# Routing of a mixture of experts in batches of tiles, the first gathers ahead of the weight splits, and a rare branch moved to the end

## The chip, the cores and the metric

The kernel runs on one core of a Trainium2 chip. The metric is the device time of one execution in microseconds (us). The engines that matter here are TensorE (PE, with its weight loads PEld), VectorE (DVE), ScalarE (ACT), GpSimd (POOL) and SyncE (SP, which here issues plain DMAs only).

## The reference

Two transformer-like blocks run one after the other on a sequence of S = 2048 rows of D = 1024. The change touches only the last part of the second: the hierarchical mixture of experts, with 4 groups of 8 experts, two experts for a row, and hidden width 256.

```python
def hierarchical_moe(h, w_rg, b_rg, w_re, b_re, w_gate, w_up, w_down):
    t = h.reshape(N, D)
    g_prob = softmax(t @ w_rg + b_rg)
    g_p, g_idx = lax.top_k(g_prob, 1)
    e_logits = (t @ w_re + b_re).reshape(N, N_GROUPS, EXPERTS_PER_GROUP)[chosen group]
    e_p, e_idx = lax.top_k(softmax(e_logits), TOP_K)
    weights = g_p * e_p / sum(e_p)
    expert = g_idx * EXPERTS_PER_GROUP + e_idx
    ...
    hid = silu(xb @ w_gate[e]) * (xb @ w_up[e])
    y[rows of e] += weights * (hid @ w_down[e])

def hybrid_layer(...):
    ...
    x = x + gate1 * (mixed @ w_out)
    h2 = rms_norm_2(x, norm2_g) * (1.0 + scale2) + shift2
    return x + gate2 * hierarchical_moe(h2, ...)
```

## The kernel before, in words

The time up to 2444 computes the first block and the attention and recurrence of the second, and is the same before and after. What follows has three parts.

**The routing stage** (`p6`, L1898) goes over the 16 tiles of 128 rows. For a tile, `operand` (L1930) splits the mixed activations into a high and a low part, `main` (L1937) multiplies them with `w_out` on PE (three products for one, L98 to L100, in a rounded 32-bit form) and adds each half of the result to the residual on DVE (L1946, four adds a tile), then normalizes the row (L1950 to L1955) and writes it to device memory, `h_d`, from which the experts gather. `router` (L1959), one tile behind, transposes the normalized rows (L1964), copies them (L1965), multiplies them with the router's weights (L1968, 16 instructions of 40 columns) and adds the bias (`lg`, L1970). `route` (L2012) then works on that one tile with some 37 small DVE instructions: the best group, the two best experts of it, their weights, and each row's rank in its expert's list, for which PE multiplies the choice with a triangular matrix (L2048) and the running count with ones (L2050). `place` (L2071) turns rank and expert into one-hot matrices R (128 x 128) and A (three groups of 128 columns: the token, and the weight's high and low part), and PE sums R times A into the lists of all experts in one PSUM bank (L2079), which has four columns for each expert: up to four blocks of 128 rows of its own.

**Between the routing stage and the experts** stands `route_end` (L2096): it counts the blocks of each expert (`nbi`, L2101 to L2105), makes the row indices `sidx` and weights `roww` from the bank (`row_lists`, L2081), the last block's index and weight of each expert (`lsidx`, `lroww`), and the number of blocks beyond four (`tli`). Then comes a branch, `If(nt > 0)` (L2128), with the lists for experts of more than four blocks, some 465 instructions, which this input does not take. `experts` (L2157) then clears five row buffers on POOL (L2167), splits the first expert's weights into high and low parts (`split_expert`, L2256: ACT casts at L2265, DVE subtracts at L2266), gathers the first two experts' rows (L2273, an indirect DMA that POOL issues) and transposes the first (L2285).

**The expert loop** (L2179 to L2202) is unrolled over 32 experts. Its order on PE, ACT, DVE and POOL is the program's own (a manual schedule); everything ahead of it is ordered by a planner that has costs and due times of each instruction. SP's queue is ordered by the planner throughout. Within an iteration, all engines load the number of the expert's blocks, `nb`, from `nbi` into a register (L2179), POOL gathers rows ahead, PE does half of the up and gate products of this expert, the turn and down product of the expert before (L2307, L2321), and the other half. A branch `If(nb > 1)` (L2198) holds the second to fourth blocks; 20 of the 32 experts don't take it. The results go to the output by a scatter that adds (L2323). Behind the loop a register load (L2203) and a loop over blocks beyond four (L2204) end the kernel; this input has none.

Of the kernel before, what the change touches and what calls it, by code (L numbers as in the profile page):

```python
# [20 lines left out]
P = 128  # L21
S = 2048
# [8 lines left out]
def f32(ap):  # L31
    return ap.bitcast(F32)
# [28 lines left out]
class Kernel:  # L61
# [11 lines left out]
    LATE = 15.5  # L73
    AHEAD = 3
# [44 lines left out]
    def build(self):  # L119
        tc, nc = self.tc, self.nc  # L120
        with ExitStack() as ctx:
            self.cst = cst = ctx.enter_context(tc.tile_pool(name="cst", bufs=1, reuse_waits="tile"))
# [1752 lines left out]
    def route_tiles(self, ctx):  # L1875
# [7 lines left out]
        self.nbi, self.tli = t("nbi", 32, dt=I32), t("tli", 40, dt=I32)  # L1883

        self.rk, self.ek, self.wk = t("rk", NT, 2, 2), t("ek", NT, 2), t("wk", NT, 2)
        self.io = t("io", P)
# [11 lines left out]
    def p6(self):  # L1898
        tc, nc, a = self.tc, self.nc, self.a
        V = nc.vector  # L1900
        with ExitStack() as ctx:

            qp = self.pools(ctx, "qp", ("cnt", "br", "v4", "r4", "rst_o", "lg", "mxl", "hT", "wr", "mx", "hx", "x1", "mxh", "sq", "sh2", "gn2"))
            t = lambda nm, *w, dt=F32, bufs=1: qp.tile([P, *w], dt, name=nm, bufs=bufs)

            cnt = t("cnt", 32, dt=F32R)
            V.memset(f32(cnt), 0.0)
# [29 lines left out]
            def main(n, mh, ml, r2):  # L1937
# [9 lines left out]
                nc.sync.dma_start(self.out[n * P:n * P + P, :], x)  # L1947
                hx = t("hx", D, bufs=2)
# [10 lines left out]
            def router(n, hx):  # L1959
# [12 lines left out]


            order = [4 * q + i for q in (3, 2, 1, 0) for i in range(4)]
# [22 lines left out]
            for i, n in enumerate(order):  # L1997
# [11 lines left out]
            router(order[-1], hx)  # L2009
            self.route_end(qp, cnt, rows)  # L2010

    def route(self, rp, n, lg, cnt, rows, first, last):  # L2012
# [3 lines left out]
        t = lambda nm, *w, dt=F32, bufs=2: rp.tile([P, *w], dt, name=nm, bufs=bufs)  # L2016
        U32 = mybir.dt.uint32

        g8, gi, gf = t("g8", 8), t("gi", 8, dt=U32), t("gf", 1)
        V.max(g8, lg[:, :8])  # L2020
        V.max_index(gi, g8, lg[:, :8])
        V.tensor_copy(gf, gi[:, 0:1])
        nm, ge, gs = t("nm", 1), t("ge", 8), t("gs", 1)
        V.tensor_scalar(nm, g8[:, 0:1], -1.0, None, op0=OP.mult)
        nc.scalar.activation(ge, lg[:, :8], AF.Exp, bias=nm, accum_out=gs)
        V.reciprocal(gs, gs)

        oh, el = t("oh", 4), t("el", 32)
        V.tensor_scalar(oh, self.io[:, :4], gf, -1e30, op0=OP.not_equal, op1=OP.mult)
        V.tensor_tensor(el.rearrange("p (g e) -> p g e", g=4), lg[:, 8:].rearrange("p (g e) -> p g e", g=4),  # L2030
                        oh[:, :, None].to_broadcast([P, 4, 8]), OP.add)
        m8, x8 = t("m8", 8), t("x8", 8, dt=U32)
        V.max(m8, el)
        V.max_index(x8, m8, el)
        e, w, d = self.ek[:, n], self.wk[:, n], t("d", 1)
        V.tensor_copy(e, x8[:, :2])
        V.tensor_tensor(d, m8[:, 0:1], m8[:, 1:2], OP.subtract)
        nc.scalar.activation(d, d, AF.Tanh, scale=0.5)
        V.tensor_scalar(gs, gs, 0.5, None, op0=OP.mult)
        V.scalar_tensor_tensor(w[:, 0:1], d, 1.0, gs, op0=OP.add, op1=OP.mult)  # L2040
        V.tensor_scalar(d, d, -1.0, 1.0, op0=OP.mult, op1=OP.add)
        V.tensor_tensor(w[:, 1:2], d, gs, OP.mult)

        M, Ms = t("M", 2, 32), t("Ms", 32, dt=F32R)
        V.tensor_tensor(M, self.io[:, None, :32].to_broadcast([P, 2, 32]), e[:, :, None].to_broadcast([P, 2, 32]), OP.is_equal)
        V.tensor_tensor(Ms, M[:, 0], M[:, 1], OP.add)
        pr = self.bank("aux")
        nc.tensor.matmul(pr[:, :32], self.low, Ms, start=True, stop=first)  # L2048
        if not first:
            nc.tensor.matmul(pr[:, :32], self.one, cnt, start=False, stop=True)  # L2050
        V.tensor_tensor(M, M, pr[:, None, :32].to_broadcast([P, 2, 32]), OP.mult)
        V.tensor_tensor(cnt, cnt, Ms, OP.add)
        vf, vi, ri = t("vf", 2), t("vi", 2, dt=I32), t("ri", 2, 2, dt=I32)
        V.tensor_reduce(vf, M, mybir.AxisListType.X, OP.add)
        V.tensor_copy(vi, vf)
        V.tensor_scalar(ri[:, 0], vi, 127, None, op0=OP.bitwise_and)
        V.tensor_scalar(ri[:, 1], vi, 7, None, op0=OP.arith_shift_right)
        rk = self.rk[:, n]
# [3 lines left out]
        V.tensor_scalar(cl, rk[:, 1], 4.0, 1000.0, op0=OP.is_ge, op1=OP.mult)  # L2062
        V.scalar_tensor_tensor(cl, e, 4.0, cl, op0=OP.mult, op1=OP.add)
        V.tensor_tensor(cl, cl, rk[:, 1], OP.add)
        wr, wl = t("wr2", 2, dt=F32R), t("wl2", 2)
        V.tensor_copy(wr, w)
        V.tensor_tensor(wl, w, f32(wr), OP.subtract)
        for k in range(2):
            self.place(rp, n, k, cl[:, k:k + 1], P, wr, wl, rows, first and k == 0, last and k == 1)

    def place(self, rp, n, k, col, w, wr, wl, rows, start, stop):  # L2071

        nc = self.nc
        R = rp.tile([P, P], F32R, name="R", bufs=2)
        nc.vector.tensor_scalar(R, self.io, self.rk[:, n, 0, k:k + 1], None, op0=OP.is_equal)
# [5 lines left out]
    def row_lists(self, rp, rows, c0, w):  # L2081

        V = self.nc.vector
        t = lambda nm, dt=F32: rp.tile([P, w], dt, name=f"{nm}{w}")
        cs = slice(c0, c0 + w)
        r, z = t("rl"), t("rz")
        V.tensor_scalar(r, rows[:, :w], -1.0, None, op0=OP.add)
        pd = rp.tile([P, 1], F32, name="pd")
        V.tensor_scalar(pd, self.pid, float(S + 1), None, op0=OP.add)
        V.tensor_scalar(z, r, 0.0, pd, op0=OP.is_lt, op1=OP.mult)  # L2090
        V.tensor_tensor(r, r, z, OP.add)  # L2091
        V.tensor_copy(self.sidx[:, cs], r)  # L2092
        V.tensor_copy(self.roww[:, cs], rows[:, w:2 * w])
        V.tensor_tensor(self.roww[:, cs], self.roww[:, cs], rows[:, 2 * w:3 * w], OP.add)
# [261 lines left out]
```

## Time and profile before

| | us |
|---|---|
| median of 3 runs | 3287.71 (3283.44 to 3288.76) |
| the profiled execution | 3284.43 |
| its span | 3282.3 |
| PE busy | 2997.3 (91%) |
| DVE busy | 2226.2 (68%) |
| ACT busy | 1533.3 (47%) |
| POOL busy | 903.8 (28%) |
| granted PE clock, mean | 0.964 |

The span is that of the profiled execution, the time from its first to its last instruction; the execution itself took 2.1 us more. Busy times are the time in which an engine had an instruction in work. In the rows below, a time in brackets is how long the engine stood idle ahead of the instruction, with the instruction, or the queue step of an engine (a name with q), that ended the idle time. "128*128 128x512" is the stationary and the moving operand of a product. [...]

### The profile page before, as it was taken

To read this page: it belongs to the slowest core of one execution; us is meant where nothing else is said; L and a number is where in the kernel's file an instruction comes from. 1 tells how busy PE (TensorE), PEld (TensorE's weight loads), DVE (VectorE), ACT (ScalarE), POOL (GpSimd) and SP (SyncE) were. 2 spreads that over 40 slices of the span, in tenths; PEclk is the share of its full clock that TensorE was granted. 3 is DMA by queue.
4 is the path that set the end of the run, shared out by engine and by line. 5 is a ranking of instruction groups with operands and counts; after the bars stand their busy time and mean duration, and the time that the engine had idled before them with its cause. 6 is when DMAs were issued, how large, how long until landed. Compare 5 with 4: busy or idle time off the path is not lost. (4 is left out here: it accounts for less than half of the span.)

```text
span 3282.3 us, 43935 instructions
## 1 busy us (share of the span) xinstructions
PE 2997.3 (91%) x14243; PEld 2403.5 (73%) x14243; DVE 2226.2 (68%) x4948; ACT 1533.3 (47%) x3020; POOL 903.8 (28%) x868
## 2 busy tenths in 40 slices
PE   7999999989998788899999789899999986999997
PEld 5778779968876667777888667687877764666665
DVE  4356764448786996537666698888877886674463
ACT  4332331146665543225555677666554543452332
POOL 0003550012223531443343553222200002342232
PEclk9999999999998899999999899999999988999999
DMA  5534557653637878684544521223253327996682
GB/s 171 181 83 145 188 186 233 213 137 115 201 104 204 250 226 263 208 268 146 154 135 130 131 90 55 82 66 91 69 192 131 129 96 269 291 347 190 172 261 42
DMA packets 411128, 545.44 MB, mean 166 GB/s; under 512 B 73953, under 2 KB 263745, under 8 KB 409826
## 3 DMA queue, kind: packets, MB, share of 16 engines
q1 hardware_dynamic: 392850, 508.41, 48.4%
q0 software_dynamic: 18000, 33.60, 4.6%
q8 instruction: 141, 2.31, 0.3%
q14 instruction: 137, 1.12, 0.1%
HBM read 393.00 MB, written 180.84 MB: 175 GB/s over the span
## 5 line engine op out<-in xcount | busy, mean ns | idle before, releaser
L98 PE MATMUL fm<-h,wh 128*128 128x512 f32 x960 | 388.0, 408 | 7.9 <-ACT ev L234 5.7
L99 PE MATMUL fm<-h,wh 128*128 128x512 f32 x960 | 384.0, 400 | 0.0
L100 PE MATMUL fm<-h,wl 128*128 128x512 f32 x960 | 381.5, 398 | 0.6 <-DVE wl L91 0.6
L98 PEld LDWEIGHTS fm<-h,wh 128*128 128x128 f32 x960 | 182.9, 191 | 47.8 <-ACT ev L234 7.7
L100 PEld LDWEIGHTS fm<-h,wl 128*128 128x128 f32 x960 | 182.5, 190 | 41.2 <-DVE wl L91 1.0
L99 PEld LDWEIGHTS fm<-h,wh 128*128 128x128 f32 x960 | 182.9, 191 | 31.8
L98 PE MATMUL mm<-wegh,xh 128*128 128x512 f32 x376 | 169.6, 451 | 25.7 <-ACT g L2299 24.6
L2321 PE MATMUL mm<-wd,st 128*128 128x512 f32 x368 | 167.3, 597 | 9.4 <-ACTq L2229 5.0
L2266 DVE TENSOR_TENSOR wegl<-wf,wegh 128x1024 fp32r<-128x1024 f32 x128 | 151.1, 1223 | 6.1
L2299 ACT ACTIVATE g<-mm 128x256 f32<-128x256 f32 x47 | 18.0, 383 | 290.3 <-PEq L2198 98.0
L91 DVE TENSOR_TENSOR tl<-tr,th 128x512 fp32r<-128x512 f32 (+2 forms) x204 | 130.8, 644 | 30.5 <-ACT th L90 29.7
L100 PE MATMUL mm<-wegh,xl 128*128 128x512 f32 x376 | 148.6, 395 | 0.0
L99 PE MATMUL mm<-wegl,xh 128*128 128x512 f32 x376 | 147.9, 393 | 0.0
L861 POOL TENSOR_TENSOR q<-q,q 64x512 fp32r<-64x512 f32 x32 | 43.3, 1355 | 366.3 <-ACT q L860 286.1
L90 ACT CAST th<-tr 128x512 fp32r<-128x512 f32 (+2 forms) x204 | 110.2, 548 | 43.6 <-PE tr L902 18.5
L2265 ACT CAST wegh<-wf 128x1024 fp32r<-128x1024 f32 x128 | 127.7, 1049 | 3.4 <-DVE nf L2108 3.2
L2321 PEld LDWEIGHTS mm<-wd,st 128*128 128x128 f32 x368 | 66.3, 190 | 79.5 <-issue 65.0
L2300 DVE SCALAR_TENSOR_TENSOR g<-g,mm 128x256 f32<-128x256 f32 x47 | 19.8, 421 | 144.7 <-ACT g L2299 144.7
L98 PEld LDWEIGHTS mm<-wegh,xh 128*128 128x128 f32 x376 | 71.3, 190 | 60.9 <-ACT g L2299 37.5
L98 PE MATMUL mm<-wo,mxh 128*128 128x512 f32 x256 | 105.1, 410 | 8.0 <-DVE x L1946 5.2
L2323 POOL DMA_INDIRECT out_y<-y,lsidx x32 | 51.6, 1613 | 193.0 <-DVEq L2198 119.7
L99 PE MATMUL mm<-wo,mxh 128*128 128x512 f32 x256 | 104.3, 407 | 0.0
(707 smaller groups left out, 9178.4 us busy)
## 6 DMA issues: line engine op xcount, KB each, us to landing
wf<-in_w_gate SPq DMA_DIRECT2D x64, 512.0 KB
wf<-in_w_up SPq DMA_DIRECT2D x64, 512.0 KB
wd<-in_w_down SPq DMA_DIRECT2D x62, 512.0 KB
wa<-in_w_ada SPq DMA_DIRECT2D x96, 256.0 KB
w<-in_w_in SPq DMA_DIRECT2D x43, 512.0 KB
g_d<-Gs SPq DMA_DIRECT2D x32, 544.0 KB
G<-g_d SPq DMA_DIRECT2D x32, 544.0 KB
x<-in_x SPq DMA_DIRECT2D x32, 512.0 KB
```

The source lines that it names most:

```text
L90: nc.scalar.copy(hi, src)
L91: nc.vector.tensor_tensor(lo, src, f32(hi), OP.subtract)
L98: mm(ps, lh, rh, start=start, stop=False)
L99: mm(ps, lh, rl, start=False, stop=False)
L100: mm(ps, ll, rh, start=False, stop=stop)
L861: nc.gpsimd.tensor_tensor(q[64:], q2[64:], f32(q[64:]), OP.subtract)
L2265: nc.scalar.copy(hi, f)
L2266: nc.vector.tensor_tensor(lo, f, f32(hi), OP.subtract)
L2299: nc.scalar.activation(g, pm[:, :256], AF.Tanh, scale=0.5)
L2300: nc.vector.scalar_tensor_tensor(g, g, 1.0, pm[:, :256], op0=OP.add, op1=OP.mult)
L2321: nc.tensor.matmul(po, st[:, k * P:k * P + P], wts[1][k][:, hs], start=k == 0, stop=k == 1)
L2323: nc.gpsimd.indirect_dma_start(out=self.out, out_offset=bass.IndirectOffsetOnAxis(ap=sidx, axis=0), in_=y, in_offset=None, compute_op=OP.a ...
```

## The change

1. Routing works in batches of tiles, 4, 4, 4, 3 and 1: `router` leaves the logits of a tile in a common tile, and `route` works on the whole batch with operands of three dimensions; two searches, one one-hot and four columns of A remain for each tile. The rank products run once for a batch, over 32 columns for each tile of it; the running counts are kept for all tiles.
2. `place` uses R and A in plain 32-bit floats instead of the rounded form, so the weight needs no low part: A has 2 x 128 columns instead of 3 x 128. The token numbers start at minus 2048, so `row_lists` has two DVE instructions instead of seven.
3. `router` of the last but one tile comes ahead of the last tile's `main`. From behind that `main` to the end of the experts, PE, ACT, DVE and POOL are in the program's order.
4. The branch for experts of more than four blocks moves from `route_end` to the end of the kernel, joined with the loop over such blocks. `lsidx`, `lroww` and `tli` are made in `route_last`, behind the first expert's transposes.
5. The first two row buffers are cleared and gathered into ahead of the other three and of the first expert's splits.
6. `nb` is loaded just ahead of its branch instead of at the start of the iteration.

```diff
+    BATCH = ((0, 4), (4, 8), (8, 12), (12, 15), (15, 16))
...
+        self.cnt = t("cnt", NT + 1, 32, dt=F32R)
...
-        nc.gpsimd.iota(self.tok, pattern=[[P, NT]], base=1, channel_multiplier=1, allow_small_or_imprecise_dtypes=True)
+        nc.gpsimd.iota(self.tok, pattern=[[P, NT]], base=-S, channel_multiplier=1, allow_small_or_imprecise_dtypes=True)
...
-                lg = t("lg", 40, bufs=2)
-                V.tensor_tensor(lg, pl[:, :40], br, OP.add)
-                self.route(qp, n, lg, cnt, rows, n == order[0], n == order[-1])
+                b = next(b for b, (lo, hi) in enumerate(self.BATCH) if lo <= i < hi)
+                lo, hi = self.BATCH[b]
+                if i == lo:
+                    lgs[b] = t("lg", 4, 40, bufs=2)[:, :hi - lo]
+                V.tensor_tensor(lgs[b][:, i - lo], pl[:, :40], br, OP.add)
+                if i == hi - 1:
+                    self.route(qp, order, lo, hi, lgs.pop(b), rows)
...
-                h2 = main(n, *cur)
-                if hx is not None:
-                    router(order[i - 1], hx)
+                if i == NT - 1:
+                    router(i - 1, hx)
+                x = main(n, *cur)
+                if i == NT - 1:
+
+                    self.given = self.ctx.enter_context(ExitStack())
+                    self.given.enter_context(tc.manual_schedule(engines={getattr(mybir.EngineType, k) for k in (
+                        "PE", "Activation", "DVE", "Pool")}))
+                h2 = norm(n, x)
+                if 0 < i < NT - 1:
+                    router(i - 1, hx)
...
+        pr = self.bank("aux")
+        nc.tensor.matmul(pr[:, :32 * B], self.low, Ms.rearrange("p b e -> p (b e)"), start=True, stop=False)
+        nc.tensor.matmul(pr[:, :32 * B], self.one, self.cnt[:, lo:hi].rearrange("p b e -> p (b e)"), start=False, stop=True)
...
+        for i in range(B):
+            R = rp.tile([P, 2, P], F32, name="R", bufs=2)
+            self.one_hot(R, rk[:, i, 0])
+            for k in range(2):
+                self.place(rp, order, lo + i, k, R[:, k], cl[:, i, k:k + 1], P, rows, lo + i + k == 0, lo + i + k == NT)
...
-        A = rp.tile([P, 3, w], F32R, name=f"A{w}", bufs=2)
-        for j, v in enumerate((self.tok[:, n:n + 1], f32(wr)[:, k:k + 1], wl[:, k:k + 1])):
+        A = rp.tile([P, 2, w], F32, name=f"A{w}", bufs=2)
+        n = order[i]
+        for j, v in enumerate((self.tok[:, n:n + 1], self.wk[:, i, k:k + 1])):
             nc.vector.tensor_scalar(A[:, j], self.io[:, :w], col, v, op0=OP.is_equal, op1=OP.mult)
-        nc.tensor.matmul(rows[:, :3 * w], R, A.rearrange("p a b -> p (a b)"), start=start, stop=stop)
+        nc.tensor.matmul(rows[:, :2 * w], R, A.rearrange("p a b -> p (a b)"), start=start, stop=stop)
...
+        V.tensor_scalar(self.sidx[:, cs], rows[:, :w], float(S), None, op0=OP.add)
         V.tensor_copy(self.roww[:, cs], rows[:, w:2 * w])
...
-        for x in self.xg + self.xo:
+        for e in range(2):
+            nc.gpsimd.memset(self.xg[e], 0.0)
+            self.gather(self.xg[e], 4 * e)
+        for x in (self.xo[0], self.xg[2], self.xo[1]):
             nc.gpsimd.memset(x, 0.0)
         wts, steps = self.split_expert(self.wf)
         for f in steps:
             f()
-        for e in range(2):
-            self.gather(self.xg[e], 4 * e)
         xt = self.expert_x(ep, self.xg[0])
+        self.route_last(ep)
         wf = self.load_expert(self.expert_src(1))
...
-                nb = nc.values_load(self.nbi[0:1, e:e + 1], min_val=0, max_val=16)
...
+            nb = nc.values_load(self.nbi[0:1, e:e + 1], min_val=0, max_val=16)
+            with tc.If(nb > 1):
+                self.expert_over(ep, wts, e, nb, 1, pm)
...
+        self.given.close()
         nt = nc.values_load(self.tli[0:1, 32:33], min_val=0, max_val=32)
+        with tc.If(nt > 0):
+            self.expert_tail(ep, nt)
```

## Rows read from the trace of the kernel before

**Rows 1.** Busy time by stretch; columns: stretch, us, each engine's busy us, PEclk, DMA share, GB/s

```profile
2444.00:2680.00 236.00, 226.07 (x1156) 187.79 (x1154) 187.86 (x742) 115.34 (x175) 0.95 (x1) 0.96 0.36 134
2677.30:2735.90 58.60, 23.32 (x93) 18.65 (x90) 42.77 (x204) 12.22 (x25) 7.98 (x8) 0.53 0.49 174
2736.00:3272.00 536.00, 489.83 (x1967) 333.45 (x1966) 308.71 (x403) 199.76 (x308) 170.14 (x121) 0.99 0.73 227
```

**Rows 2.** Waits of PE in the routing stage, 2444 to 2680: total, times, longest

```profile
PE mm L98 <- DVE x L1946: 5.2, 4, 3.3
```

**Rows 3.** PE in order of time through the seam: start us, us, instruction, idle before

```profile
2676.68 0.40 PE L99 MATMUL mm<-wo,mxh 128*128 128x512 f32 x1
2676.91 0.40 PE L100 MATMUL mm<-wo,mxl 128*128 128x512 f32 x1
...
2692.25 1.09 PE L1964 MATMUL tr<-ident,hx 128*128 128x128 f32 x4
2694.02 1.12 PE L1964 MATMUL tr<-ident,hx 128*128 128x128 f32 x4 [0.68 <-ACT hT L1965]
...
2698.52 3.61 PE L1968 MATMUL aux<-wr,hT 128*128 128x40 f32 x16
...
2734.11 1.94 PE L2285 MATMUL tr<-ident,xg 128*128 128x128 f32 x8 [16.51 <-DMA xg<-h_d,sidx]
2735.88 0.80 PE L98 MATMUL mm<-wegh,xh 128*128 128x512 f32 x1
```

**Rows 4.** DVE in order of time through the seam

```profile
2679.58 3.49 DVE L2266 TENSOR_TENSOR wegl<-wf,wegh 128x1024 fp32r<-128x1024 f32 x3
2682.98 0.75 DVE L1946 SCALAR_TENSOR_TENSOR x<-mm,r,x 128x512 f32<-128x512 f32 x1
...
2702.31 0.20 DVE L1970 TENSOR_TENSOR lg<-aux,br 128x40 f32<-128x40 f32 x1
...
2709.31 0.20 DVE L1970 TENSOR_TENSOR lg<-aux,br 128x40 f32<-128x40 f32 x1
...
2716.52 0.34 DVE L2078 TENSOR_SCALAR A<-io,cl,wl 128x128 fp32r<-128x128 f32 x1
...
2727.54 0.29 DVE L2091 TENSOR_TENSOR rl<-rl,rz 128x128 f32<-128x128 f32 x1 [5.86 <-DVEq L2128]
2727.87 0.68 DVE L2092 CAST sidx<-rl 128x128 int32<-128x128 f32 x1
...
2745.79 3.50 DVE L2266 TENSOR_TENSOR wegl<-wf,wegh 128x1024 fp32r<-128x1024 f32 x3
```

**Rows 5.** POOL in order of time, two issues of a gather

```profile
2729.45 1.23 POOL L2273 DMA_INDIRECT xg<-h_d,sidx  x1 [0.98 <-DVE lc L2116]
...
2745.85 2.03 POOL L2273 DMA_INDIRECT xg<-h_d,sidx  x1 [0.30 <-issue]
```

**Rows 6.** PE in order of time: a down product, and the head of an expert

```profile
2748.95 3.60 PE L2321 MATMUL mm<-wf,st 128*128 128x512 f32 x8
...
2756.00 0.47 PE L98 MATMUL mm<-wegh,xh 128*128 128x512 f32 x1 [0.71 <-ACT g L2299]
```

**Rows 7.** Waits of PE in the expert loop, 2736 to 3283: total, times, longest

```profile
PE mm L98 <- ACT g L2299: 24.6, 29, 2.1
```

**Rows 8.** Line 2179, register loads: queue, operation, count, ns min/median/max, first and last start

```profile
L2179 SPq TENSOR_LOAD <-nbi x32: 263/263/491, 2714.3 to 2737.2; - x32
...
L2179 PEldq TENSOR_LOAD <-nbi x32: 297/303/416, 2734.1 to 3253.3; - x32
```

**Rows 9.** Line 2203, the register load behind the expert loop

```profile
L2203 PEldq TENSOR_LOAD <-tli x1: 305/305/305, 3266.5 to 3266.5; - x1
```

**Rows 10.** The end in order of time, PE and POOL

```profile
3266.51 3.70 PE L2321 MATMUL mm<-wd,st 128*128 128x512 f32 x8 [0.53 <-ACT st L2309]
...
3271.28 1.57 POOL L2323 DMA_INDIRECT out_y<-y,lsidx  x1 [7.40 <-DVEq L2204]
```

**Rows 11.** Line 2204, the last loop's waits on SP's queue

```profile
L2204 SPq EVENT_SEMAPHORE  x19: 17/28/28, 3195.3 to 3277.9; - x19
```

More of the change, by code (lines that the diff above doesn't have):

```diff
@@ L2008, in p6, with route @@
                     self.wf = self.load_expert(self.expert_src(0), True)
-            router(order[-1], hx)
-            self.route_end(qp, cnt, rows)
-    def route(self, rp, n, lg, cnt, rows, first, last):
+            router(NT - 1, hx)
+            self.route_end(qp, rows)
+    def route(self, rp, order, lo, hi, lg, rows):
         nc = self.nc
         V = nc.vector
-        t = lambda nm, *w, dt=F32, bufs=2: rp.tile([P, *w], dt, name=nm, bufs=bufs)
+        B = hi - lo
+        t = lambda nm, *w, dt=F32: rp.tile([P, 4, *w], dt, name=nm)[:, :B]
+        bc = lambda x, *w: x.to_broadcast([P, B, *w])
+        X = mybir.AxisListType.X
@@ L2030, in route @@
[L2030 to L2038, printed above, removed]
+        gm, eq, e1, ge = t("gm"), t("eq", 4), t("e1"), t("ge", 4)
@@ new lines, in route @@
+        V.tensor_copy(e, x8[:, :, :2])
+        M, Ms = t("M", 2, 32), t("Ms", 32, dt=F32R)
+        V.tensor_tensor(M.rearrange("p b k e -> p (b k) e"), self.io[:, None, :32].to_broadcast([P, 2 * B, 32]),
+                        e.rearrange("p b k -> p (b k)")[:, :, None].to_broadcast([P, 2 * B, 32]), OP.is_equal)
+        V.tensor_tensor(Ms, M[:, :, 0], M[:, :, 1], OP.add)
+        for i in range(B):
+            V.tensor_tensor(self.cnt[:, lo + i + 1], f32(self.cnt)[:, lo + i], f32(Ms)[:, i], OP.add)
@@ L2063, in route @@
         V.scalar_tensor_tensor(cl, e, 4.0, cl, op0=OP.mult, op1=OP.add)
[L2064 to L2071, printed above, removed]
+        V.tensor_tensor(cl, cl, rk[:, :, 1], OP.add)
@@ L2083, in row_lists @@
+    def row_lists(self, rows, c0, w):
         V = self.nc.vector
-        t = lambda nm, dt=F32: rp.tile([P, w], dt, name=f"{nm}{w}")
         cs = slice(c0, c0 + w)
[L2086 to L2092, printed above, removed]
+        V.tensor_scalar(self.sidx[:, cs], rows[:, :w], float(S), None, op0=OP.add)
@@ L2093, in row_lists, with route_end @@
         V.tensor_copy(self.roww[:, cs], rows[:, w:2 * w])
-        V.tensor_tensor(self.roww[:, cs], self.roww[:, cs], rows[:, 2 * w:3 * w], OP.add)
-    def route_end(self, rp, cnt, rows):
+    def route_end(self, rp, rows):
         tc, nc = self.tc, self.nc
@@ L2105, in route_end, with route_last @@
         V.tensor_scalar(self.nbi, ci, 7, None, op0=OP.arith_shift_right)
-        self.row_lists(rp, rows, 0, P)
+        self.row_lists(rows, 0, P)
+    def route_last(self, rp):
+        V = self.nc.vector
+        t = lambda nm, *w, dt=F32: rp.tile([P, *w], dt, name=nm)
+        nf, one, lc, sel, sv = t("nf", 32), t("one1", 32), t("lc", 32), t("sel", 32, 4), t("selv", 32, 4)
         V.tensor_copy(nf, self.nbi)
-        lc, sel, sv = t("lc", 32), t("sel", 32, 4), t("selv", 32, 4)
         V.tensor_scalar(lc, nf, 1.0, 4.0, op0=OP.max, op1=OP.min)
@@ L2203, in experts @@
-        nt = nc.values_load(self.tli[0:1, 32:33], min_val=0, max_val=32)
+        for e in range(32):
+            self.gather(self.xo[0], 4 * e + 1)
+            if e < 30:
+                self.gather(self.xg[(e + 2) % 3], 4 * e + 8)
+            wn, steps = self.split_expert(wf) if e < 31 else (None, [])
+            split = lambda: steps and steps.pop(0)()
+            pm = self.mmps()
+            self.expert_up(pm, wts, xt, range(4))
+            s = self.expert_gate(ep, last[0]) if last else None
+            for _ in range(3):
+                split()
+            st = self.expert_turn(ep, s) if last else None
+            xn = self.expert_x(ep, self.xg[(e + 1) % 3]) if e < 31 else None
+            split()
+            if last:
+                self.expert_down(ep, last[1], st, last[2])
+            self.expert_up(pm, wts, xt, range(4, 8))
+            if e < 30:
+                wf = self.load_expert(self.expert_src(e + 2))
+            nb = nc.values_load(self.nbi[0:1, e:e + 1], min_val=0, max_val=16)
+            with tc.If(nb > 1):
+                self.expert_over(ep, wts, e, nb, 1, pm)
+            last = pm, wts, (self.lsidx[:, e:e + 1], self.lroww[:, e:e + 1])
+            wts, xt = wn, xn
```

175 lines of the change are left out of this document (83 added, 92 removed).

## The prediction

> **What bounds the kernel now.** I read the busy table by stretches first. [...] In PE's order of time the last product of the last tile ends at 2677.31 (2676.91 + 0.40) and the first expert product starts at 2735.88 [rows 3]: 58.6 us, in which PE is busy 23.3 and mostly at half clock (mean 0.53) [rows 1]. Nothing there is limited by an engine's speed; it is a chain of small steps. In the expert loop, 2736 to 3272, PE is busy 489.8 of 536 us at 0.99 [rows 1], so PE bounds again, and its largest wait is 24.6 us in 29 pieces at the head of an expert's products [rows 7]. So each part is priced in the stage where it acts.
>
> **Routing in batches.** DVE needs 7.0 us before the change for one routed tile (logits at 2702.31 and again at 2709.31, with nothing idle between) [rows 4]. A batch of four does some 40 small instructions at about 0.2 us of pitch (8 us) and, per tile, two searches, the one-hot, four columns of A at 0.26 and a count, some 2.2 us: about 16.8 us for four, 4.2 a tile. DVE saves some 40 us in all, but DVE is not the bound here. On PE the placement grows: it was two products of 384 columns in the rounded form, which at the 0.23 us between products of 512 columns (2676.68 to 2676.91) [rows 3] are 0.17 us each; now it is two of 256 columns in full F32, and full-F32 products of 512 columns take 0.45 us an instruction, two instructions each (3.60 us for 8) [rows 6], so about 0.45 for 256. That is +0.56 us a tile, +8 for 15 tiles; the rank products, issued five times instead of 16, give back about 1.4: **+6.6 us** of PE. [...] A later DVE, free of 40 us, makes the adds of L1946 sooner, but a batch also holds DVE for longer in one piece, so I take back 6. Net **+1**; bounds: all 15 come back, -8; none does and the pieces cost 3 more, +10.
>
> **The seam.** Before, behind the last product came: three weight splits of expert 0 on DVE (3.49 us from 2679.58) that held back the last add (2682.98) [rows 4]; the rest of three tiles' routing in turn, each with 16 logit products of 3.61 us at half clock (2698.52) [rows 3]; the last columns of A until 2716.86; three weight splits of expert 1; and 5.86 us in which DVE stood at the not-taken long branch, with row_lists split around it (2727.54) [rows 4]. Then the gather was issued (2729.45) [rows 5] and landed for transposes at 2734.11 [rows 3].
> After, only tile 15 is left. From the end of its product I sum: tile 14's router moved in front, 2.9 (transposes of 1.09 and 1.12 and logits of 3.61 at half clock, halved); add 0.3 + 0.75; norm from the add's end to the first transpose, 2683.73 to 2692.25, less 1.0 for the other tiles' routing between its steps: 7.5; transposes from 2692.25 to 2695.14 with the copy and hand-over behind them, 4.1; logits 3.6 + 0.4; one route alone, 2709.31 to 2716.86, 7.5 [rows 3, 4]; placement 0.9 (two of 0.45), count product 0.4, block counts and sidx 1.3 (four small steps, 0.68 for sidx among them as it was); gather from the index to landing 2728.55 to 2734.11, 5.5; transposes to the first product 1.8 [rows 3, 4]. That is 37.0, and with 1.0 for the gather (below) 38.0 against 58.6: **-21**. Bounds: the batch 12 to 14 may reach into the seam, and DVE's order may delay tile 15 by 9, so -12; if norm, transposes and route lose another fifth without such steps between, -26. The four splits of expert 0 (3.49 for three on DVE, so 1.2 each [rows 4]) now run in the gather's shadow of 5.5; should that cover be short, the first product waits for one split, 1.2. Expert 1's splits and the 14 small steps for lsidx move into the first iteration, where DVE has room: 308.7 of 536 us busy [rows 1]; 0 to +1.
> The gathers issued ahead now run beside DVE's splits. Issue by POOL took 1.23 us with DVE free (2729.45) and 2.03 beside splits (2745.85, over splits from 2745.79 to 2749.29) [rows 4, 5]: +1.0, the one in the sum. [...]
>
> **The register load.** At 29 boundaries of the loop PE stands before the next expert's first product, 24.6 us together [rows 7], 0.85 each; where no branch is taken 0.71, as at 2756.00 [rows 6]. The load of nb sits in this gap: 0.303 us on PE's queue, 32 times [rows 8]; with its dispatch about 0.41 (an estimate: a third more for the steps around it). Now it stands behind the last products, ahead of the branch that already was there. That such a load runs ahead of the array the end shows: L2203 was loaded on PE at 3266.5 [rows 9] while products went on to 3270.2 [rows 10]. 29 x 0.41 = **-12**; bounds -9 (the bare 0.303) and -14 (all but 0.37 of each gap), or 0 if it isn't hidden (rival 3). On DVE, ACT and POOL the load moves as well; ACT is busy 199.8 of 536 [rows 1], so nothing waits longer. SP's loads (32 of 0.263, each with two steps more) ran in one row from 2714 to 2737 [rows 8]; what is queued behind them on SP are the weight loads, see the rivals.
>
> **The end.** The not-taken long branch goes behind the last scatter. Its 5.86 us stand beside the landing of that scatter: issued at 3271.28 [rows 10], the final waits end at 3277.9 [rows 11]. So 0; bounds -1 and +4. [...]
>
> **Sum.** +1 - 21 - 12 + 0 = -32. The profiled execution took 3284.43 us, 3.3 below the median 3287.71. From the profiled time 3252.4, on the median's scale 3255.7; I take 3255. The forecast's own range is 3238 to 3270.
>
> **Rivals.** 1, the seam gives half: the order on PE, ACT, DVE and POOL is written by hand from the last tile's norm on, so one late step holds all behind it, and route of tiles 12 to 14 may spill some 12 us of DVE into tile 15's norm; for it speaks DVE's 42.8 of 58.6 us in the seam [rows 1]. Then -9 instead of -21, **3267**. 2, SP is not in the hand-made order: its 32 register loads (about 20 us in a row) stand ahead of expert 1's weights, and the second expert waits; against it, in steady state weights are issued far ahead. +8, **3264**. 3, the change doesn't do what it says: the load still waits for the array, for the wait for the gate lies in the same gap [rows 7]; -20 only, **3268**. [...] 5, **slower**: the batches hold DVE in pieces of 16 us where a tile of PE's work lasts 14.7 (236/16), the residual adds wait, PE's result buffers fill and PE stops. It decides from 8 us per batch: four batches are 32 and eat up all the rest; at 9 each, **3292**. Against it: DVE's order here is planned with due times, so adds pass between the small steps, and DVE has 48 us free.
>
> **How the numbers follow.** Forecast 0.62, rival 1 0.14, 2 0.07, 3 0.06, 4 0.04, 5 0.04, unnamed 0.03. The range 3237 to 3273 takes in the forecast with its bounds and rivals 1 to 4. A measurement of this kernel can tell about 0.2%, 6.6 us, from no change: faster means below 3281. All but rival 5, and far corners where the seam and the loop both fail, lie below: 0.91 faster, 0.05 same, 0.04 slower.
>
> **What would show it.** Right: the last product of the last tile to the first expert product takes 36 to 41 us; no DVE wait for the branch before sidx; PE's waits at the heads of experts fall from 24.6 to about 12; placement instructions twice as many, PE's idle in the routing stage not over 10. Wrong: PE waits for L1946 of several us in each batch; the seam over 47; a gap of 0.7 that stays although the register load has left it; the second expert's products waiting for weights.

## The result and the profile after

The changed kernel takes **3246.18 us** (median of 4 runs, 3240.00 to 3247.80) against 3285.57 for the kernel before in its 4 runs: ratio 0.9878, interval 0.9859 to 0.9896, so 39 us faster. The forecast was 3255, between 3237 and 3273. A second set of runs of the same kernel (below) gave 0.987 (0.9849 to 0.989). The sum was near; its terms were not. To see that, both profiled executions are cut at the same events: the first and the last product with `w_out`, the first and the last product of the experts. The stretches are: the routing stage, the seam, the expert loop and the end. Here is the table of busy time by stretch, first of the kernel before, then of the changed one (columns as in [rows 1]; PEclk is the granted clock, TensorE's clock as a share of its full speed):

```profile
2431.20:2677.30 246.10, 237.20 (x1199) 197.19 (x1200) 190.20 (x742) 118.69 (x176) 0.95 (x1) 0.96 0.40 145
2677.30:2735.88 58.58, 23.30 (x93) 18.63 (x90) 42.75 (x204) 12.22 (x25) 7.98 (x8) 0.53 0.49 174
2735.88:3270.20 534.32, 489.94 (x1967) 333.57 (x1966) 308.08 (x402) 199.76 (x308) 169.42 (x120) 0.99 0.74 227
3270.20:3282.30 12.10, 0.01 (x1) 0.00 (x0) 0.75 (x1) 0.00 (x0) 1.57 (x1) 0.71 0.26 40
```

```profile
2423.70:2659.30 235.60, 235.60 (x1219) 197.76 (x1220) 162.01 (x462) 85.20 (x124) 0.95 (x1) 0.99 0.41 151
2659.30:2695.72 36.42, 18.49 (x83) 14.85 (x81) 25.03 (x115) 9.34 (x16) 7.19 (x6) 0.66 0.59 209
2695.72:3229.10 533.38, 493.80 (x1967) 333.63 (x1966) 310.31 (x420) 202.56 (x311) 176.70 (x122) 0.99 0.75 233
3229.10:3238.20 9.10, 0.01 (x1) 0.00 (x0) 0.75 (x1) 0.00 (x0) 1.57 (x1) 0.76 0.36 55
```

| stretch | before | after | difference | forecast |
|---|---|---|---|---|
| ahead of the routing stage | 2431.2 | 2423.7 | -7.5 | 0 |
| routing stage | 246.1 | 235.6 | -10.5 | +1 |
| seam | 58.6 | 36.4 | -22.2 | -21 |
| expert loop | 534.3 | 533.4 | -0.9 | -12 |
| end | 12.1 | 9.1 | -3.0 | 0 |
| span | 3282.3 | 3238.2 | -44.1 | -32 |

The first line is no gain: up to 2392 PE's instructions are the same ones in the same order, and in the runs of this study the routing stage began anywhere from 2423.7 to 2433.8. Of the 9.9 us between the spans of the changed kernel's two profiled executions, 7.1 lie here. This is why single stretches are compared below, and why two kernels that are 5 us apart can't be told by their medians. In the profiled execution the changes themselves make -36.6.

**The routing stage** has PE busy without a gap, 235.6 of 235.6 us, at a clock of 0.99 instead of 0.96: the 8.9 us of idle are gone, the wait for L1946 [rows 2] among them.

**The seam** in PE's order of time (columns as in [rows 3]):

```profile
2664.32 0.63 PE L1974 MATMUL tr<-ident,hx 128*128 128x128 f32 x4 [1.13 <-DVE hx L1964]
...
2669.50 0.45 PE L2073 MATMUL aux<-Ms,low 128*128 128x96 f32 x1 [3.16 <-DVE Ms L2069]
2669.75 3.60 PE L1978 MATMUL aux<-wr,hT 128*128 128x40 f32 x16
...
2677.22 2.08 PE L2121 MATMUL aux<-A,R 128*128 128x256 f32 x4 [3.65 <-DVE A L2120]
...
2693.95 1.94 PE L2331 MATMUL tr<-ident,xg 128*128 128x128 f32 x8 [7.54 <-DMA xg<-h_d,sidx]
2695.72 0.80 PE L99 MATMUL mm<-wegh,xh 128*128 128x512 f32 x1
```

and DVE's part of it, from the last add to the row lists and the splits behind them:

```profile
2659.36 0.75 DVE L1952 SCALAR_TENSOR_TENSOR x<-mm,r,x 128x512 f32<-128x512 f32 x1 [2.03 <-PE mm L101]
...
2673.39 0.20 DVE L1983 TENSOR_TENSOR lg<-aux,br 128x40 f32<-128x40 f32 x1 [3.26 <-PE aux L1978]
...
2686.99 0.28 DVE L2127 TENSOR_SCALAR sidx<-aux 128x128 int32<-128x128 f32 x1
...
2687.39 4.62 DVE L2312 TENSOR_TENSOR wegl<-wf,wegh 128x1024 fp32r<-128x1024 f32 x4
```

The last product ends at 2659.3. The norm now goes straight through: 4.2 us from the add's end to the first transpose, against 8.5 in [rows 3, 4]. Then PE stands 3.16 us for `Ms` of the batch of tiles 12 to 14, which is ahead of the last tile's logits in the program's order; and from the logits (2673.39) to `sidx` (2686.99) DVE works 13.6 us, since it routes that batch and the last tile together. No branch is on the way; the splits (2687.39) lie behind the row lists. The first gather beside them:

```profile
2688.17 1.54 POOL L2319 DMA_INDIRECT xg<-h_d,sidx  x1 [55.82 <-DMA wd<-in_w_down]
...
2690.96 1.94 POOL L2319 DMA_INDIRECT xg<-h_d,sidx  x1 [0.28 <-POOL xg L2205]
```

From its issue to the transposes 5.8 us pass, 4.7 before [rows 3, 5]. So the +1.0 for a gather beside splits is near in this execution, but not by its reason: the issue itself is only 0.31 longer (1.54 against 1.23), and the rest lies between the issue and the transposes. In the other runs whose first gather is issued beside splits, issue to transposes takes 5.5 to 8.1 us; in e5 and e6 below, where no split runs beside it, 4.7 and 4.8. Whether the splits lengthen it or the weight transfers of the same time was not tried. The issue did not wait for the splits to end: it was over at 2689.71, while DVE's four splits ran until 2692.01.

**The expert loop** is where 11 us are missing. A head is PE's idle time ahead of an expert's first product. The heads did get shorter where nothing else is late. Two heads, the second and the third expert's (columns as in [rows 6]):

```profile
2706.20 0.47 PE L99 MATMUL mm<-wegh,xh 128*128 128x512 f32 x1 [1.76 <-DVEq L2236]
...
2716.79 0.47 PE L99 MATMUL mm<-wegh,xh 128*128 128x512 f32 x1 [0.30 <-PEq L2236]
```

The third expert's head is 0.30 instead of 0.71: the 0.41 that was forecast, to the digit; where the branch's body was run it is 0.54 instead of 0.94. But others are 0.8 to 1.8, and the sum of PE's waits at the heads is 17.0 instead of 25.7 (24.6 of these are in [rows 7]):

```profile
PE mm L99 <- PEq L2236: 6.9, 16, 1.5
PE mm L99 <- ACT g L2345: 5.8, 10, 0.8
...
PE tr L2331 <- DMA xg<-h_d,sidx: 1.0, 2, 0.8
...
PE mm L99 <- DVEq L2236: 4.3, 4, 1.8
...
PE tr L2331 <- DMA xo<-h_d,sidx: 3.6, 2, 1.9
```

**The end** is 3.0 us shorter. The branch, now L2243, does stall DVE there, for 2.9 us from 3229.5 (first and last start in each row):

```profile
L2243 DVEq COMPARE_BRANCH  x1: 56/56/56, 3229.5 to 3229.5; - x1
...
L2243 DVEq EVENT_SEMAPHORE  x1: 21/21/21, 3232.4 to 3232.4; - x1
```

It lies beside the last scatter, issued at 3230.18, which has the engines wait until 3236.6, as forecast. The 3 us come from elsewhere: the loop over blocks beyond four is now inside the branch, so its own start and end are passed over. From the scatter's landing to the span's end it took 4.9 us before and takes 1.6 now. Before, every engine's queue went through the loop's waits behind the landing (1.3 us, [rows 11] for SP's), and only then could POOL begin the step that ends its queue (DRAIN), which took 2.8 us. Now that step begins at 3231.7, beside the landing, and is over 0.8 us behind it. POOL's step before and after (count, ns min/median/max, first and last start; the longest is the first):

```profile
L2352 POOLq DRAIN  x3: 46/103/2763, 3278.7 to 3282.0; - x3
```

```profile
L2398 POOLq DRAIN  x3: 46/113/5731, 3231.7 to 3238.0; - x3
```

In all thirteen profiled runs with the branch around that loop the end is 8.9 to 9.3 us, in e5 too, whose long list of instructions is not there but in the seam.

### The profile page after: what moved, and what is told of

The parts are those of the page before. It is cut to its first block, busy times and chain, and to the rows that moved or that the text cites. A ratio compares the mean times of both kernels' runs of the same rounds, so it can differ in the third digit from the quotient of the medians.

```text
span 3238.2 us, 43471 instructions
## 1 busy us (share of the span) xinstructions
PE 2990.6 (92%) x14254; PEld 2399.5 (74%) x14254; DVE 2183.7 (67%) x4596; ACT 1500.7 (46%) x2962; POOL 909.7 (28%) x869
## 5 line engine op out<-in xcount | busy, mean ns | idle before, releaser
L91 ACT CAST th<-tr 128x512 fp32r<-128x512 f32 (+2 forms) x204 | 110.1, 548 | 42.5 <-PE pj L101 18.3
```

What stands on the lines that cost most here:

```text
L91: nc.scalar.copy(hi, src)
```

## The experiments

Two questions were open: why the routing stage gained 10 us, and where the loop's 12 us went. The stretches of all profiled runs, cut as above (us; heads: PE's idle ahead of an expert's products; y: DVE's waits for a result buffer, where the profile names a scatter that still reads it; each stretch is from the one profiled execution of its run):

| run | stage | seam | loop | heads | y | median | ratio to before |
|---|---|---|---|---|---|---|---|
| before | 246.1 | 58.6 | 534.3 | 25.7 | 11.3 | 3285.6 | 1 |
| changed | 235.6 | 36.4 | 533.4 | 17.0 | 14.4 | 3246.2 | 0.9878 (0.9859 to 0.9896) |
| a0_after | 235.6 | 36.7 | 535.7 | 19.3 | 13.5 | 3247.4 | 0.9870 (0.9849 to 0.9890) |
| e1_nb_start | 235.4 | 36.2 | 537.9 | 26.5 | 14.5 | 3247.8 | 0.9873 (0.9854 to 0.9891) |
| e2_single | 242.9 | 40.9 | 535.5 | 18.5 | 16.2 | 3259.7 | 0.9907 (0.9888 to 0.9926) |
| e3_f32r | 235.1 | 36.1 | 529.1 | 16.1 | 12.1 | 3240.7 | 0.9843 (0.9820 to 0.9867) |
| e4_pair_last | 235.6 | 34.9 | 535.1 | 18.9 | 14.0 | 3246.3 | 0.9877 (0.9857 to 0.9896) |
| e8_light_late | 235.6 | 36.1 | 523.4 | 15.8 | 0.8 | 3240.5 | 0.9861 (0.9840 to 0.9881) |
| e9_light_start | 235.6 | 37.4 | 537.2 | 29.2 | 0.8 | 3249.6 | 0.9898 (0.9877 to 0.9920) |
| e10_y3 | 235.6 | 37.9 | 522.9 | 14.4 | 0 | 3237.7 | 0.9859 (0.9838 to 0.9880) |
| e5_if_back | 234.1 | 39.2 | 528.9 | 17.6 | 17.6 | 3243.3 | 0.9863 (0.9845 to 0.9882) |
| e6_auto_seam | 235.4 | 38.0 | 526.7 | 16.4 | 17.2 | 3241.8 | 0.9864 (0.9841 to 0.9886) |
| e11_best | 235.0 | 38.5 | 526.4 | 15.2 | 0 | 3242.6 | 0.9861 (0.9842 to 0.9879) |
| e12_gather_last | 235.6 | 36.0 | 536.3 | 18.3 | 16.3 | 3243.1 | 0.9861 (0.9844 to 0.9877) |

The medians of the three sets stand each beside their own runs of before (3287.6, 3284.2 and 3290.1), so the ratios are compared, not the medians. How far a stretch varies by itself is seen where an edit does not touch it: the stage is 235.4 to 235.6 us in the seven runs that route alike and keep the order (changed, a0, e1, e8, e9, e10, e12), but the seam is 36.1 to 37.9 in the first six of them (mostly the first gather, 5.5 to 8.1 us), and the loop is 533.4 to 536.3 in changed, a0 and e12. Differences of up to 2 us in a seam or 3 in a loop can't be told from this scatter.

**a0_after.** No edit.

> The changed kernel once more, to see which stretches repeat. [...]

Stage and seam repeat to 0.3 us. The loop takes 535.7. PE again waits for late rows of a second block, 1.5 us at 68 us into the loop and 2.4 at 226, and slow products follow both, so the loss belongs to the changed kernel. In the first execution the waits were 1.9 and 1.6 us, with slow products behind the first alone. That one looks so (PE in order of time, then the stretch before it and the stretch from there):

```profile
2761.79 1.13 PE L2331 MATMUL tr<-ident,xo 128*128 128x128 f32 x8 [1.92 <-DMA xo<-h_d,sidx]
```

```profile
2758.00:2764.00 6.00, 3.44 (x20) 2.42 (x18) 2.98 (x6) 1.74 (x4) 2.19 (x2) 0.90 1.07 393
2764.00:2770.00 6.00, 6.00 (x9) 2.62 (x9) 1.22 (x2) 0.00 (x0) 0.46 (x1) 0.53 0.78 201
```

PE waits for the rows of an expert's second block, then the clock stands at 0.53 for the down products: they take 5.9 us instead of 3.0, so 2.9 us are lost by the clock on top of the 1.9 of waiting.

**e1_nb_start.**

```diff
         for e in range(32):
+            nb = nc.values_load(self.nbi[0:1, e:e + 1], min_val=0, max_val=16)
...
-            nb = nc.values_load(self.nbi[0:1, e:e + 1], min_val=0, max_val=16)
             with tc.If(nb > 1):
```

> The block count is loaded at the start of each iteration again, all else as in the changed kernel. Theory A: the load's 0.41 us at each of 30 heads is real and was won, and what the loop lost stands elsewhere (first iteration, gathers, clock); then PE's waits at the heads grow from 17 to 27 to 29 us and the loop takes 11 to 13 us longer than in the changed kernel run beside it. Theory B: the loop is bounded by something else, weight transfers above all, so that a gap closed at the head opens elsewhere; then the heads grow by 12 but the loop is within 3 us.

The heads are back at 26.5, but the loop is only 2.2 to 4.5 us longer than in the two executions of the changed kernel, and the median 0.4: nearer to theory B. Its loop is also 3.6 us longer than the one before the change with the same heads. Against that one it loses 4.2 us in its first three experts and no more behind them, so the changed start of the loop has a price of its own.

**e8_light_late and e9_light_start**, the same pair with a third of the expert weights' transfers left out of the loop:

```diff
         for i in range(6):
+            if i >= 4 and not first and len(keep) == 2:
+                fs.append(keep[i - 4])
+                continue
```

> The changed kernel without the down weights' transfers from the third expert on (it uses those of the second expert again, so its result is another): a third of the expert weights' bytes is left out and nothing else. To be read with the next one, which differs by the place of the load of the block count alone. Theory A: where the changed kernel's loop gained nothing, the DMA engines are full (share 0.99 to 1.03 from 2800 to 2920) and a scatter of results lands late, DVE's add for the next waits for its buffer and the head with it; then the loop is 522 to 528 us here, against 533 to 536. Theory B: the lost time is PE's own (fetch of code, clock), and the loop stays at 532 to 536.

> As the one before, with the block count loaded at the start of each iteration. Theory A: with the DMA engines eased the late load is worth its 0.41 us at nearly every head: this loop takes 9 to 13 us longer than that of the one before. Theory B: it takes only 2 to 4 us longer, as the pair with all weights (537.9 against 533.4 and 535.7).

The pair differs by 13.8 us (523.4 against 537.2), where with all weights it differed by 2.2 to 4.5. With the load at the start, easing the DMA engines gives nothing (537.2 against 537.9): that loop is PE's. With the late load it gives 10 to 12. Theory A in both (13.8 is just above its range). The late load is worth its 30 x 0.41 = 12 or a little more, and the transfers keep it back. The loops of the two, in the table by stretch:

```profile
2705.10:3228.50 523.40, 488.43 (x1967) 332.14 (x1966) 308.25 (x420) 202.94 (x311) 168.72 (x123) 1.00 0.65 183
```

```profile
2696.70:3233.90 537.20, 490.12 (x1967) 333.90 (x1966) 313.18 (x420) 202.75 (x311) 166.37 (x121) 0.99 0.64 177
```

**e10_y3** asks by which way.

```diff
-        y = ep.tile([P, D], F32, name="y", bufs=2)
+        y = ep.tile([P, D], F32, name="y", bufs=3)
```

> Three result buffers y instead of two, all else as in the changed kernel. Theory A: DVE's add waits for a buffer that a scatter still reads (14.4 us in 8 waits in the changed kernel, 3.7 us at 2903), and the head after it is late; with a third buffer these waits are gone and the loop takes 528 to 531 us. Theory B: a scatter waits for the one before it anyway (POOL waits 21.4 us for that), so a third buffer only moves the wait; the loop stays at 532 to 536.

The loop falls to 522.9, below theory A's range, with all transfers in it, DMA share 0.76 as against 0.75:

```profile
2703.90:3226.80 522.90, 490.55 (x1967) 332.89 (x1966) 308.85 (x420) 202.69 (x311) 164.27 (x121) 0.99 0.76 236
```

So it is not the bytes as such but what waits for them. DVE's waits for a buffer that a scatter reads, in the changed kernel, in e1 and in e8 (there is none in e10):

```profile
DVE y L2368 <- DMA out_y<-y,lsidx: 14.4, 8, 3.2
DVE y L2368 <- issue: 8.0, 4, 2.6
```

```profile
DVE y L2368 <- DMA out_y<-y,lsidx: 14.5, 13, 2.1
```

```profile
DVE y L2374 <- DMA out_y<-y,lsidx: 0.8, 1, 0.8
```

The line was in the profile of before too (11.3 us in 12 waits, none over 2.1). With the load at the head of an iteration these waits end before PE needs DVE, in e1 13 of them at most 2.1 us long. With the late load PE is 0.4 us earlier at every expert and the waits grow, 8.0 us of them under "issue", which e1 and e10 don't have. One of these and the head behind it, in DVE's and in PE's order of time in the changed kernel:

```profile
2895.66 1.41 DVE L2368 SCALAR_TENSOR_TENSOR y<-mm,lroww,g2b 128x512 f32<-128x512 f32 x2 [2.51 <-issue]
```

```profile
2897.27 0.47 PE L99 MATMUL mm<-wegh,xh 128*128 128x512 f32 x1 [0.82 <-DVEq L2236]
```

The add waits 2.51 us, DVE passes the branch of L2236 only behind it, and PE's head, released by that step of DVE's queue, is 0.82 instead of 0.30. The heads account for 2.6 to 4.9 of the 10.5 to 12.8 us that e10's loop is shorter. Another 6.0 to 7.6 lie at the two experts whose second block's rows came late, the sixth and the nineteenth: from the head to the first product of the second block the changed kernel takes 20.6 and 17.3 us, a0 18.7 and 20.8, e10 15.8 and 16.1. This is the same buffer by another way. In POOL's queue the gather of those rows stands behind the scatter of the result before, which waits for DVE's add. POOL in order of time, in the changed kernel (PE starts the sixth expert at 2749.31) and in e10 (at 2756.85):

```profile
2749.26 1.61 POOL L2369 DMA_INDIRECT out_y<-y,lsidx  x1 [6.11 <-DVEq L2236]
2751.18 1.45 POOL L2319 DMA_INDIRECT xo<-h_d,sidx  x1 [0.31 <-issue]
```

```profile
2754.86 1.61 POOL L2369 DMA_INDIRECT out_y<-y,lsidx  x1 [5.39 <-DVEq L2236]
2756.92 1.03 POOL L2319 DMA_INDIRECT xo<-h_d,sidx  x1 [0.45 <-PEq L2236]
```

The gather is issued 1.9 us behind the head with two buffers and 0.1 with three. In the ten runs with the late load and all weights, PE's wait for these rows follows the end of that issue: over 3.3 us behind the head (changed, a0, e2, e5, e12) it waits 1.5 to 1.9, at 1.8 to 2.2 (e3, e4, e6) 0.9 to 1.2, at 1.0 to 1.1 (e10, e11, three buffers) at most 0.2. At the nineteenth expert the order is looser: the issue ends 4.6 us behind the head in seven of these runs, with waits of 0.5 to 2.6. So e5 and e6 have a late gather too. Against these two e10 is 6 to 8 us shorter from the second expert on.

**e2_single.**

```diff
-    BATCH = ((0, 4), (4, 8), (8, 12), (12, 15), (15, 16))
+    BATCH = tuple((i, i + 1) for i in range(16))
```

> Batches of one tile each: the routing's instructions of the changed kernel, run 16 times on one tile. Theory A: the stage's 10 us came from batching, which takes some 45 us of small steps off DVE; then PE's idle in the routing stage comes back to 6 to 10 us, its mean clock to about 0.96, and the stage takes 243 to 247 us instead of 235.6. Theory B: it came from the shorter placement (four columns of A instead of six, no low part of the weight); then the stage stays within 2 us of 235.6. The seam: tile 14 is then routed alone ahead of the last tile's work, so it may be 2 to 4 us shorter.

Nearer to theory A, though its three numbers are missed, each by a little or more: the stage takes 242.9, with PE idle for 4.0 us in it at a clock of 0.98, and its old wait is back, 3.3 us in one piece:

```profile
PE mm L99 <- DVE x L1952: 3.3, 1, 3.3
```

```profile
2431.60:2674.40 242.80, 238.85 (x1230) 200.09 (x1231) 183.87 (x729) 105.58 (x157) 0.95 (x1) 0.98 0.41 146
```

So batching makes 7.3 of the stage's 10.5 us; the other 3 were not tried by themselves. The guess on the seam was wrong: 40.9, not shorter. The routing instructions of the changed kernel, run on one tile at a time, make the whole kernel 12 us slower than in batches.

**e3_f32r** takes the rounded placement back, with its third group of columns and two parts of the weight.

```diff
-            R = rp.tile([P, 2, P], F32, name="R", bufs=2)
+            R = rp.tile([P, 2, P], F32R, name="R", bufs=2)
...
-        A = rp.tile([P, 2, w], F32, name=f"A{w}", bufs=2)
+        A = rp.tile([P, 3 if three else 2, w], F32R if three else F32, name=f"A{w}", bufs=2)
```

> The placement in the rounded form again, three groups of columns and a weight in two parts, all else (batches too) as in the changed kernel. Theory A: plain F32 costs PE 0.28 us a product (0.45 against 0.17), so the rounded form takes 7 to 9 us off PE in the routing stage; with DVE still free of most of its small steps the stage takes 227 to 230 us, and the seam is within 2 us. Theory B: the two extra columns of A for each tile and choice (0.26 us of DVE each, 32 of them, 8 us) hold DVE, PE waits instead, and the stage stays at 234 to 237.

The stage stays at 235.1: B's number without B's reason, for PE is busy without a gap (235.1 of 235.1). The placement did get shorter, 20 products within the stage from 7.7 to 4.6 us (start to start), but the clock stood at 0.97 instead of 0.99, and why it did is not shown. The stage in e3, then in a0:

```profile
2433.80:2668.90 235.10, 235.10 (x1199) 197.48 (x1200) 167.68 (x490) 85.40 (x124) 0.95 (x1) 0.97 0.41 151
```

```profile
2430.80:2666.40 235.60, 235.58 (x1219) 198.03 (x1220) 162.01 (x462) 85.24 (x124) 0.96 (x1) 0.99 0.41 151
```

In its loop the two gathers are less late (PE waits 0.9 and 0.5 us for them), 529.1, which is most of its better median; nothing in the edit touches the loop, so this is not counted as its effect.

**e4_pair_last.**

```diff
-    BATCH = ((0, 4), (4, 8), (8, 12), (12, 15), (15, 16))
+    BATCH = ((0, 4), (4, 8), (8, 12), (12, 14), (14, 16))
```

> Batches (12, 14) and (14, 16) instead of (12, 15) and (15, 16): only one routing of two tiles lies behind the last product, not one of three and one of one. Theory A: in the seam the batch of three stands on the last tile's way (PE waits 3.2 us for its Ms ahead of the last tile's logits, and DVE works for both from 2673.4 to 2684.8); then the seam falls from 36.5 to 31 to 33 us and the stage stays within 2 us of 235.6. Theory B: the last tile's own chain of norm, logits, route and gather sets the seam, and the other batch fills its gaps; then it stays at 35.5 to 37.5.

34.9, between the two: the 3.2 us wait is gone, and some of it comes back as two tiles' routing in a row. `sidx` is made 1.3 to 2.2 us sooner behind the last product than in the runs with the old batches.

**e5_if_back** puts the branch ahead of the first gather.

```diff
+        self.route_last(ep)
+        nt = nc.values_load(self.tli[0:1, 32:33], min_val=0, max_val=32)
+        with tc.If(nt > 0):
+            self.tail_lists(ep)
         for e in range(2):
             nc.gpsimd.memset(self.xg[e], 0.0)
```

> The long branch with its lists stands ahead of the first gather again (with the steps for lsidx and tli that it needs), all else as in the changed kernel; the loop over blocks beyond four stays behind a branch at the end. Theory A: the branch costs its stall on the way to the gather, 5.9 us before, plus the 3 us of the steps in front of it and the register load, so the seam grows from 36.5 to 44 to 47 us, and the loop's first experts get back some 1 to 2 us. Theory B: the stall belongs to DVE's old order and POOL passes the branch at once; then the seam grows by 3 to 4 only.

39.2, nearly B (2.4 to 2.8 us more than in the changed kernel). DVE stalls 4.13 us, with its splits behind the stall, while POOL goes on with the gather:

```profile
2697.24 4.63 DVE L2314 TENSOR_TENSOR wegl<-wf,wegh 128x1024 fp32r<-128x1024 f32 x4 [4.13 <-DVEq L2206]
```

```profile
2695.39 1.23 POOL L2321 DMA_INDIRECT xg<-h_d,sidx  x1 [0.34 <-POOL xg L2209]
```

The gather is issued 5.5 us behind `sidx` instead of 0.9, for DVE's steps of `route_last` (3.1 us), the register load and the clearing of the row buffer now stand ahead of it. But no split runs beside it, and from its issue to the transposes 4.7 us pass instead of 5.8 and 7.0. So the 2.4 to 2.8 are a balance of both. The stall itself is not on the way: the splits behind it are done at 2701.87, as PE begins its first product (2701.89). And the loop's start is better: with the steps of `route_last` done, the second expert's head is 0.3 us instead of 1.8 and 3.1.

**e6_auto_seam** opens the program's own order at the expert loop, as before the change.

```diff
-                if i == NT - 1:
-                    self.given = self.ctx.enter_context(ExitStack())
...
         last = None
+        self.given = self.ctx.enter_context(ExitStack())
```

> The planner orders the seam again; the program's order begins with the expert loop, as before the change. All else as in the changed kernel. Theory A: most of the seam's 22 us come from what is on the way (one tile's routing, no branch, splits behind the gather), and the planner, which put weight splits ahead of the last add and of the row lists before, gives back 3 to 8 us of it: seam 40 to 44. Theory B: the order alone is worth nothing, 36 to 37.5.

38.0: much nearer to B, and within 0.1 of the longest seam with the hand-made order (37.9 in e10). Again two things balance: the planner puts the splits ahead of the last add, so `sidx` comes 2.6 to 3.5 us later behind the last product than in the changed kernel's runs, but the gather has no split beside it (4.8 us to the transposes). The loop with the hand-made order is the dearer one by 7 to 9 us; 1.4 to 2.8 of them lie at the second expert's head (0.3 us here). The rest is not shown to be the order's: e3's loop, with the hand-made order, was 529.1.

**e12_gather_last.**

```diff
+        for x in self.xg + self.xo:
+            nc.gpsimd.memset(x, 0.0)
         wts, steps = self.split_expert(self.wf)
...
+        for e in range(2):
+            self.gather(self.xg[e], 4 * e)
```

> The clearing of all five row buffers and the first expert's splits ahead of the gathers in the program's order, all else as in the changed kernel. Theory A: the splits are on DVE and ACT behind the row lists in either case, and POOL can clear the buffers while it waits, so the place of the gathers is worth under 1 us: seam 36 to 37.5. Theory B: POOL's clearing waits for the buffers' former users and holds the gathers, 2 to 4 us: seam 38 to 41.

36.0, theory A: the place of the gathers in the program is worth nothing here (36.4 and 36.7 in the two executions of the changed kernel). The gathers and the clearing are POOL's work, the splits DVE's and ACT's; when each began in e12 is not shown.

**e11_best** joins the edits of e3, e4 and e10, clears both row buffers first, and moves `route_last` behind the first expert's products.

> Three result buffers, batches (12, 14) and (14, 16), the placement in the rounded form, the steps for lsidx behind the first expert's products instead of ahead of the second expert's splits, and both row buffers cleared ahead of the first gather. Theory A (the gains add up): loop 519 to 522 us, since the 1.4 us that the first iteration lost come back too, seam 32 to 35, stage 235; the median is 10 to 14 us below the changed kernel's 3246 to 3247. Theory B: what is won at the loop's start is lost to the next late transfer: loop 523 to 526, 6 to 9 us below.

Theory B, and worse: loop 526.4, seam 38.5. It loses 2.3 us in the first expert and 1.7 at the second, where the head is now 4.0 us; after that it is level with e10. With `route_last` behind the last split of that iteration, DVE reaches the first branch only at 2714.9, 0.4 us ahead of the second expert's first product. No version is shown to be faster than the changed kernel by its ratio. From the start of the routing stage on, in one profiled execution each, e10 takes 805.5 us, e3, e6 and e11 809, the changed kernel 814.5 and 817.3. So e10 is the one to take, on this evidence alone.

## Why the prediction was right, and which steps of it failed

- **Direction and size**: -32 forecast, -39 measured, within the range. Two terms were wrong by 11 each and cancelled, so that the total came near is luck; of the large terms only the seam's held.
- **The seam**, -21: -22.2, and 36.4 us against the forecast 38.0. Its parts moved more than its sum. Less than forecast: the end of the last add comes 0.8 us behind the last product, where 4.0 were put down for tile 14's router and the add, since that router runs in the norm's shadow; and the norm took 4.2 and not 7.5, for little interleaves with it any more. More than forecast: the batch of three tiles did spill over, as rival 1 had it. It adds 1.3 to the last tile's transposes (3.2 us of waiting on PE), and from the logits to the end of `sidx` it takes 13.9 us where route, placement, counts and `sidx` were put at 10.1. That the gain comes from what is on the way is read from this chain; e6 and e12 leave little of it to the order by hand and none to the earlier place of the gathers, and e5 puts the branch with its steps at 2.4 to 2.8 us there, with the stall itself off the way. No run brings back the 22 us by undoing one part.
- **Routing in batches**, +1: -10.5. The step that failed is "so I take back 6": all 8.9 us of idle went, and the clock rose from 0.96 to 0.99. Of the 15 us in this term's bounds, 9.9 are the idle time of [rows 1]; no run shows the other 5, the author's estimate for the clock. e2 shows that batching does most of it (7.3). The placement term of +8 was mis-sized as well: 20 of the 32 products lie within the stage, where a plain one took 0.39 us and not 0.45, and a rounded one (in e3) 0.23 and not 0.17; it is +3 there. Rival 5, DVE held in long pieces, is refuted: PE has no gap in that stage.
- **The register load**, -12: the price of 0.41 held, and e8 against e9 agrees with its sum (13.8). The step that failed is "so nothing waits longer", which looked at ACT's busy time. With two result buffers a late scatter already held DVE in the loop, hidden under the heads; shortening the heads uncovered it, at the heads and in the gathers behind the scatter on POOL (e10). The load's move alone is worth 2.2 to 4.5 us there (e1), little more than the loop's own scatter. That was neither rival 3, for the heads did fall, nor rival 2: no expert waited for its weights.
- **Moved into the first iteration**, "0 to +1": 2 to 4. DVE has room as a mean of the loop, but not in that iteration: the third expert's products start 21.1 and 22.7 us into the loop, and 19.0 and 18.8 in e5 and e6, where these steps are elsewhere or ordered by the planner.
- **The end**, 0: -3.0, for the loop that is passed over with the branch, which was not priced: the prediction took 3277.9 for the end, and the span went on to 3282.3. The stall itself is covered, as forecast.

## What to carry to other kernels

A gap on the bounding engine that is closed pays only up to the next wait beside it: read the waits of the engines that feed it (here DVE for a result buffer, 11 us, each of them hidden) before the gap is counted as gain, and give that resource one more buffer in the same change. Small steps done for several tiles at once pay through the waits of the engine that they hold up (here 7.3 us of the stage, e2), even where their own engine is not the bound. Work that is moved to "an engine with room" must be laid beside that engine's busy time in the very stretch that it is moved to (here 2 to 4 us in the loop's first iteration).

## What was not expected of the hardware

In e5 the branch over the long body that is not run stalled the engines unequally: DVE stood for 4.13 us, and POOL passed it and issued a gather at 2695.39, 1.9 us ahead of DVE's next step. The body there holds instructions of DVE and PE and none of POOL. At the end of the changed kernel the same branch had DVE stand for 2.9 us.

And short waits of PE in the expert loop were followed by a low clock in some cases only. Of the waits of 1.5 us and more at heads and for rows, these had a low granted clock over the next 5 to 7 us: 2.06 us (before the change; 0.67), 1.92 (changed; 0.60), 3.1, 1.5 and 2.4 (a0; 0.68, 0.69 and 0.57). It stayed at 1.00 after 1.76, 1.52 and 1.64 (changed). So waits of 1.5 us went either way. In the execution before the change and in that of the changed kernel the low clock cost some 1.7 and 3.4 us on top of the wait (an estimate: one less the granted clock, 0.89 and 0.77, times the 15 us behind the wait).
